# Two operand distances and one step of the FFN's order in a float32 decoder block

## The chip, the cores and the metric

The kernel runs on one core of a Trainium2 chip. The metric is the device time of one execution in microseconds; before the change the median of three runs is 378.98 us. The matrix engine is called PE or TensorE here, its weight loads PEld, the vector engine VectorE or DVE, the scalar engine ScalarE or ACT.

## What is computed

One decoder layer over 256 tokens of width 1024, in float32, cut to what matters:

```python
h = rms_norm(x, attn_norm_g)
proj = h @ w_in                      # qa ka va qb kb vb (512 columns each), 8 forget logits, 2048 gate logits
o_a = moba_attention(rope(norm(qa)), rope(norm(ka)), va)     # 8 heads of 64; one block of 256 keys: causal attention
o_b = forgetting_attention(norm(qb), norm(kb), vb, log_f)    # 8 heads, with a cumulative decay in the scores
gates = sigmoid(g_logit + b_gate)
x = x + (gates[0] * (o_a @ w_branch_moba) + gates[1] * (o_b @ w_branch_fox)) @ w_out
u, g = split(rms_norm(x, ffn_norm_g) @ w_ffn_up)             # 2 x 2816 columns
g = causal_depthwise_conv(g, ffn_conv_w) + ffn_conv_b        # width 3
x = x + (silu(g) * u) @ w_ffn_down
```

## The kernel before

**Products in three matmuls.** Every operand of a large product is split into two float32r tiles, a high part and a rest; a product is high × high, rest × high and high × rest. The splitting of weights is `load`: it fetches a chunk of 1 MB into `raw` (a ring of RB = 3 buffers), then for each half of the chunk ScalarE copies the high part to `whi` (L124) and VectorE subtracts for `wlo` (L125); both have rings of HB = 6 slots of 4096 bytes a partition. `use(c, h)` asks for a half, and lets `load` run AHEAD = 5 halves in front. Chunks are fetched in the order of the list `chunks`; all weights' fetches are issued on one queue (SP).

**Which operand is stationary.** A matmul holds one tile of 128 columns in the array (loaded by PEld) and streams the other past it.
- `project_lead` (L225) and `project` (L235), which make q, k, v: x (`xh`, `xl`) is stationary, 512 columns of `whi` or `wlo` are streamed.
- `twin` (L445 to L447), for the gates and for `up` of the FFN; the branch projections (L541 to L543); the output projection (L568 to L570); `down` (L637 to L639): the weights are stationary, 256 columns of activations are streamed. These stand in `xh`, `xl`, `oh`, `ol` and, for `down`, in `qA`, `qB`, `kA`, which belong to the attention before.
- the norm of the FFN (L596): `onesr` stationary, `sqr` streamed.

**Addresses.** Tiles lie in SBUF one behind the other as they are first named. `gap0` of GAPS[0] bytes, the twelve slots of `whi` and `wlo`, and `onesr` come first, then `gap1` of GAPS[1] bytes, then x's tiles, `oh`, `ol`, `qA`, `qB`, `kA` and `sqr`, all of sizes that are multiples of 1024 bytes. The slots start at 4384 (32 modulo 256) and `xh` at 54240 (224 modulo 256). All slices taken for a matmul start at multiples of 512 bytes from there, so streamed minus stationary is 192 modulo 256 wherever weights are stationary, 64 where x is, and 0 in the scores of the attention (`qA` or `qB` against `kA`, L385, L386).

**Order.** PE runs in the order in which the program names its matmuls; the other engines follow their data. The attention's small steps (transposes L280 and L408, scores L385 and L386, values L419) are put between the projections and the gates by hand. In the FFN, `up(f)` makes 128 columns of u and of g in 48 matmuls, `activate(f)` brings them from PSUM (L606) through the convolution and silu to the tiles that `down` streams (L618, L619), and `down(p)` takes two such f in 48 matmuls. `norm2` runs inside `up(1)`, so that `activate(0)` and `activate(1)` come after it. The order of the steps is u0 u1 u2 u3 d0 u4 u5 d1 u6 u7 d2 and so on. `down` holds five of the eight PSUM banks, which leaves three for `up`.

Of the kernel before, what the change touches and what calls it, by code (L numbers as in the profile page):

```python
# [9 lines left out]
F32R = mybir.dt.float32r  # L10
# [7 lines left out]
P = 128  # L18
S = 256
NT = 2  # L20
D = 1024
KT = D // P
HD = 64
NH = 8
W4 = 512
DFF = 2816
NF = DFF // P
# [2 lines left out]
HALF = 8  # L30
RB, HB, AHEAD = 3, 6, 5
NWARM = 9
GAPS = (160, 192)
LW = S + 2 * W4


C_G2, C_BG, C_CW, C_CB, C_QG, C_BF, C_GR = 0, 8, 24, 90, 112, 116, 124
C_END = 156


@with_exitstack
def decoder_block(ctx, tc, a, out):
# [7 lines left out]
    def T(shape, tag, bufs=1, dt=F32):  # L50
        return sb.tile(shape, dt, tag=tag, bufs=bufs, name=tag)

    def bank():
        return ps.tile([P, 512], F32, tag="bank", bufs=8, name="bank")


    def gap(tag, n):
        nc.gpsimd.memset(T([P, n // 4], tag), 0.0)

    gap("gap0", GAPS[0])  # L60
    for tag in ("whi", "wlo"):
        T([P, 1024], tag, HB, F32R)
    T([P, P], "onesr", 1, F32R)
    gap("gap1", GAPS[1])
    for tag in ("xh", "xl", "oh", "ol"):
        T([P, KT, S], tag, 1, F32R)
# [8 lines left out]
    chunks = [("lead", j) for j in range(2)] + [("qkv", 0, 1), ("qkv", 1, 1)]  # L75
# [1 line left out]
    chunks += [("wg", c) for c in range(KT)]  # L77
    chunks += [("wb", c) for c in range(4)]
    chunks += [("wo", c) for c in range(4)]
    for j in range(NF // 2):  # L80
        chunks += [("wu", 2 * j), ("wu", 2 * j + 1)]
        if j > 0:
            chunks.append(("wd", j - 1))
    chunks.append(("wd", NF // 2 - 1))
    pos = {c: i for i, c in enumerate(chunks)}
    split = {}
    state = {"next": 0, "raw": None}

    def load(upto):
        while state["next"] <= min(upto, 2 * len(chunks) - 1):  # L90
            i, h = divmod(state["next"], 2)
            c = chunks[i]
            if h == 0:
                raw = state["raw"] = T([P, 2 * LW], "raw", RB)
                if c[0] == "lead":
                    cuts = (0, S + W4, LW, LW + S + W4, 2 * LW) if i == 0 else (0, LW, 2 * LW)
                else:
                    cuts = (0, 1024, 2048) if i < 4 else (0, 2048)
                src = a[c[0]]
                for j in c[1:]:  # L100
                    src = src[j]
                if i == 2:
                    nc.sync.dma_start(xT[:, 4:8], a["xT"][:, 4:8])
                for u, v in zip(cuts, cuts[1:]):
                    nc.sync.dma_start(raw[:, u:v], src[:, u:v])
            hi = T([P, 1024], "whi", HB, F32R)
            lo = T([P, 1024], "wlo", HB, F32R)
            if c[0] == "lead":
                k = 2 * i + h
                piece = state["raw"][:, h * LW:(h + 1) * LW]  # L110
                xk, raw = piece[:, 0:S], piece[:, S:]
                split_x(k, xk)
                nc.scalar.activation(xsq[0][:, k], xk, AF.Square)
                n = 2
            else:
                raw = state["raw"][:, h * 1024:(h + 1) * 1024]
                n = 1
                if i == 2:
                    for k in (4 + 2 * h, 5 + 2 * h):
                        split_x(k, xT[:, k])  # L120
            w = 1024 // n
            for j in range(n):
                s = slice(j * w, (j + 1) * w)
                nc.scalar.activation(hi[:, s], raw[:, s], AF.Copy)  # L124
                nc.vector.tensor_tensor(lo[:, s], raw[:, s], hi[:, s].bitcast(F32), op=ALU.subtract)  # L125
            split[c, h] = (hi, lo)
            state["next"] += 1

    def use(c, h):
        load(2 * pos[c] + h + AHEAD)  # L130
        if c == ("wb", 0) and h == 0:
            nc.sync.dma_start(xT[:, 0:4], a["xT"][:, 0:4])
        return split.pop((c, h))


    sm = T([P, C_END], "sm")
    g1 = T([P, KT], "g1")
    nc.scalar.dma_start(g1, a["g1"])

    def col(c, n=1):  # L140
        return sm[:, c:c + n]
# [7 lines left out]
    def split_x(k, x):  # L149
        g = g1[:, k:k + 1]  # L150
        if k == 0:
            nc.vector.tensor_scalar_mul(xh[:, k], x, g)
        else:
            nc.scalar.activation(xh[:, k], x, AF.Copy, scale=g)
        nc.vector.scalar_tensor_tensor(xl[:, k], x, g, xh[:, k].bitcast(F32), op0=ALU.mult, op1=ALU.subtract)
# [11 lines left out]
    load(5)  # L167
    nc.sync.dma_start(sm, a["smalls"])
    nc.scalar.activation(xsq[1], xT[:, 4:8], AF.Square)
    xss = T([P, 3, 512], "bias")  # L170
    nc.gpsimd.tensor_tensor(xss[:, 0], xsq[0][:, 0:2].rearrange("p k t -> p (k t)"), xsq[0][:, 2:4].rearrange("p k t -> p (k t)"), op=ALU.add)
    nc.gpsimd.tensor_tensor(xss[:, 1], xsq[1][:, 0:2].rearrange("p k t -> p (k t)"), xsq[1][:, 2:4].rearrange("p k t -> p (k t)"), op=ALU.add)
    nc.gpsimd.tensor_tensor(xss[:, 2], xss[:, 0], xss[:, 1], op=ALU.add)
# [6 lines left out]
    ones = cst[:, 256:384]  # L180
    mask3 = cst[:, 384:768]
    cos2 = cst[:, 768:832].rearrange("p (t c) -> p t c", t=NT)
    onesr = T([P, P], "onesr", 1, F32R)
    nc.scalar.activation(onesr, ones, AF.Copy)
    wfr = T([P, KT, NH], "wfr")
    nc.sync.dma_start(wfr, a["wf"])
# [30 lines left out]
    V = T([P, NT, 2 * W4], "V")  # L217
# [77 lines left out]
    bias = T([P, NH, 384], "bias")  # L295
# [129 lines left out]
    gates = T([P, KT, 2, S], "gates")  # L425
# [107 lines left out]
    for c in range(4):  # L533
        bp = banks()
        for br in range(2):
            wh, wl = use(("wb", c), br)
            for j in range(2):
                o = bp[j][:, br * S:(br + 1) * S]
# [5 lines left out]
        for j in range(2):  # L544
            b = 2 * c + j
# [12 lines left out]
    for c in range(4):  # L558
        for h in range(2):
            wh, wl = use(("wo", c), h)  # L560
            j = 2 * (c % 2) + h
            for i in range(2):
                b = 2 * j + i
                o = acc[b]
                for k4 in range(4):
                    k = 4 * (c // 2) + k4
# [32 lines left out]
    def up(f):  # L599
        up_ = bank()  # L600
        twin("wu", f, up_, hh, hl, f == 0, norm2 if f == 1 else None)
        return up_

    def activate(f, up_):
        ev = T([P, 2, S], "sq", 2)
        nc.vector.tensor_tensor(ev, up_.rearrange("p (b t) -> p b t", b=2), rs2[:, None, :].to_broadcast([P, 2, S]), op=ALU.mult)  # L606
        u, g = ev[:, 0], ev[:, 1]
        w = T([P, 3, S], "s", 3)
        cv, sl, av = w[:, 0], w[:, 1], w[:, 2]
        nc.scalar.activation(cv, g, AF.Identity, scale=col(C_CW + 2 * NF + f), bias=col(C_CB + f))  # L610
        nc.vector.scalar_tensor_tensor(cv[:, 1:], g[:, 0:S - 1], col(C_CW + NF + f), cv[:, 1:], op0=ALU.mult, op1=ALU.add)
        nc.vector.scalar_tensor_tensor(cv[:, 2:], g[:, 0:S - 2], col(C_CW + f), cv[:, 2:], op0=ALU.mult, op1=ALU.add)
        nc.scalar.activation(sl, cv, AF.Silu)
        nc.vector.tensor_tensor(av, u, sl, op=ALU.mult)
        if f % 2 == 0:
            acts[f // 2] = T([P, 4, S], ("qA", "qB", "kA")[f // 2 % 3], 1, F32R)
        ah, al = acts[f // 2][:, f % 2], acts[f // 2][:, 2 + f % 2]
        nc.scalar.activation(ah, av, AF.Copy)  # L618
        nc.vector.tensor_tensor(al, av, ah.bitcast(F32), op=ALU.subtract)  # L619
# [4 lines left out]
    def down(p):  # L624
        ac = acts.pop(p)
        last = p == NF // 2 - 1
        w2 = [use(("wd", p), h) for h in range(2)]
        order = [(h, d) for d in ((0, 1), (2, 3), (4, 5), (6,), (7,)) for h in range(2)] if last else [(h, (d,)) for h in range(2) for d in range(KT)]
        for h, ds in order:
            wh, wl = w2[h]  # L630
            ah, al = ac[:, h], ac[:, 2 + h]
            for d in ds:
                b = 4 if d == 7 else d // 2
                c = d % 2 if d < 6 else 0
                o = acc[b][:, c * S:(c + 1) * S]
                w = slice(d * P, (d + 1) * P)
                nc.tensor.matmul(o, wh[:, w], ah, start=(p == 0 and h == 0 and c == 0), stop=False)  # L637
                nc.tensor.matmul(o, wh[:, w], al, start=False, stop=False)  # L638
                nc.tensor.matmul(o, wl[:, w], ah, start=False, stop=(last and h == 1 and d == ds[-1]))  # L639
            if last and h == 1:  # L640
                n = len(ds)
                y = yy[:, ds[0]:ds[0] + n]
                nc.vector.tensor_tensor(y, acc[b][:, 0:n * S].rearrange("p (b t) -> p b t", b=n), x1[:, ds[0]:ds[0] + n], op=ALU.add)
                nc.sync.dma_start(out[:, ds[0]:ds[0] + n], y)

    for j in range(NF // 2):
        pair = []
        for f in (2 * j, 2 * j + 1):
            pair.append(up(f))
            if j > 0:  # L650
                activate(f, pair.pop())
        if j == 0:
            for f in range(2):
                activate(f, pair[f])
        if j > 0:
            down(j - 1)
    down(NF // 2 - 1)


def _layout(i):  # L660
# [19 lines left out]
    a["wd"] = c(i["w_ffn_down"][0].reshape(NF // 2, 2, P, D).transpose(0, 2, 1, 3).reshape(NF // 2, P, 2048))  # L680
    sm = np.empty((P, C_END), f)
    a["g1"] = c(i["attn_norm_g"][0].reshape(KT, P).T)
# [42 lines left out]
```

## Time and profile before

| | us |
|---|---|
| runs | 378.75, 378.98, 379.49 |
| the profiled execution | 379.49 |
| its span, first to last instruction | 377.7 |
| PE busy in it | 370.6 |
| DVE busy | 288.8 |
| ACT busy | 228.9 |
| mean granted TensorE clock | 1.000 |

The profile is of one execution, and its span leaves out what lies around the first and the last instruction. A matmul's own duration in it is partly modelled and spans more than two of its neighbours' starts; the pace is read from start to start, in the timeline, or from the count of matmuls in a stretch of the windows view. In views that name what waited, `L638 <- DVE qA L619` means that the matmul of line 638 began when the vector engine's instruction of line 619 had written `qA`.

### The profile page before, as it was taken

The page shows a single profiled execution, that of the slowest core. Times are in us where ns is not written, and L with a number is a line of the kernel's source. Part 1 is how long each engine was busy: PE and PEld are TensorE (multiplying, and loading weights), DVE is VectorE, ACT ScalarE, POOL GpSimd, SP SyncE. Part 2 cuts the span into 40 slices and gives each one's busy share as a digit, 9 for nine tenths or more (in the row PEclk, how much of TensorE's full clock was granted, in tenths as well). Part 3 has the DMA queues.
Part 4 walks back from the last instruction along what each step waited for, and adds up shares of the span by engine and source line. Part 5 has one row for each costly group of instructions (what it writes and reads, how often), then busy time and mean ns, then how long its engine had stood idle before and what let it go on. Part 6 is the DMA issues. An engine that isn't in the chain of part 4 may idle for free.

```text
span 377.7 us, 7097 instructions
## 1 busy us (share of the span) xinstructions
PE 370.6 (98%) x2893; PEld 349.4 (93%) x2893; DVE 288.8 (76%) x509; ACT 228.9 (61%) x387; POOL 15.4 (4%) x19
## 2 busy tenths in 40 slices
PE   8999999999899999999999999999999999999996
PEld 4787888889799989999999899999999999999996
DVE  4989989898997663886795978686766867677653
ACT  5947696759957794445577755555454646455430
POOL 2430000000000000000050000000000000000000
PEclk9999999999999999999999999999999999999999
DMA  8976622655156334454544545555564565546002
GB/s 268 411 268 252 252 111 95 241 193 209 52 217 211 125 113 150 186 183 159 217 162 174 219 147 194 222 180 172 208 222 164 180 215 210 175 179 220 0 2 111
DMA packets 11424, 68.63 MB, mean 182 GB/s; under 512 B 1528, under 2 KB 1920, under 8 KB 3968
## 3 DMA queue, kind: packets, MB, share of 16 engines
q1 hardware_dynamic: 11088, 67.13, 49.5%
q10 hardware_dynamic: 304, 1.06, 0.7%
q8 instruction: 22, 0.36, 0.4%
q14 instruction: 10, 0.08, 0.1%
HBM read 67.13 MB, written 1.06 MB: 181 GB/s over the span
## 4 chain that ended last, share of the span: by engine, by line
PE 73%; DVE 10%; ACT 9%; issue 3%; DMA 3%; SPq 0%; ACTq 0%; DVEq 0%
PE bank L445 13%; PE bank L447 12%; PE bank L446 12%; PE bank L638 5%; PE bank L639 5%; DVE wlo L125 5%; PE bank L637 5%; PE bank L235 4%; ACT whi L124 3%; PE bank L541 2%; PE bank L542 2%; PE bank L569 2%; PE bank L568 2%; PE bank L570 2%; PE bank L543 2%
## 5 line engine op out<-in xcount | busy, mean ns | idle before, releaser
L125 DVE TENSOR_TENSOR wlo<-raw,whi 128x1024 fp32r<-128x1024 f32 (+1 forms) x126 | 153.3, 1221 | 49.4 <-ACT whi L124 48.9
L124 ACT ACTIVATE whi<-raw 128x1024 fp32r<-128x1024 f32 (+1 forms) x126 | 128.7, 1029 | 82.3 <-PE bank L446 47.5
L445 PE MATMUL bank<-oh,whi 128*128 128x256 f32 x352 | 97.5, 277 | 0.0
L446 PE MATMUL bank<-ol,whi 128*128 128x256 f32 x352 | 97.5, 277 | 0.0
L447 PE MATMUL bank<-oh,wlo 128*128 128x256 f32 x352 | 97.5, 277 | 0.0
L446 PEld LDWEIGHTS bank<-ol,whi 128*128 128x128 f32 x352 | 66.2, 188 | 0.0
L445 PEld LDWEIGHTS bank<-oh,whi 128*128 128x128 f32 x352 | 66.2, 188 | 0.0
L447 PEld LDWEIGHTS bank<-oh,wlo 128*128 128x128 f32 x352 | 66.1, 188 | 0.0
L445 PE MATMUL bank<-xh,whi 128*128 128x256 f32 x128 | 36.3, 284 | 0.4 <-DVE qB L292 0.4
L447 PE MATMUL bank<-xh,wlo 128*128 128x256 f32 x128 | 35.7, 279 | 0.0
L446 PE MATMUL bank<-xl,whi 128*128 128x256 f32 x128 | 35.7, 279 | 0.0
L445 PEld LDWEIGHTS bank<-xh,whi 128*128 128x128 f32 x128 | 24.1, 189 | 1.5 <-issue 0.7
L235 PE MATMUL bank<-whi,xh 128*128 128x512 f32 x80 | 25.4, 399 | 0.0
L235 PE MATMUL bank<-wlo,xh 128*128 128x512 f32 x80 | 25.0, 394 | 0.2 <-DVE wlo L125 0.2
L235 PE MATMUL bank<-whi,xl 128*128 128x512 f32 x80 | 24.9, 392 | 0.0
L446 PEld LDWEIGHTS bank<-xl,whi 128*128 128x128 f32 x128 | 24.1, 188 | 0.0
L447 PEld LDWEIGHTS bank<-xh,wlo 128*128 128x128 f32 x128 | 24.1, 188 | 0.0
L606 DVE TENSOR_TENSOR sq<-bank,rs 128x512 f32<-128x512 f32 x22 | 15.1, 690 | 6.5 <-PE bank L447 6.5
L638 PE MATMUL bank<-qA,whi 128*128 128x256 f32 x64 | 17.8, 278 | 0.9 <-DVE qA L619 0.9
L235 PEld LDWEIGHTS bank<-wlo,xh 128*128 128x128 f32 x80 | 15.0, 188 | 3.9 <-DVE wlo L125 0.6
L394 ACT ACTIVATE s<-s,nm 128x128 f32<-128x128 f32 (+1 forms) x32 | 14.2, 448 | 6.6 <-DVE nm L391 6.6
L235 PEld LDWEIGHTS bank<-whi,xl 128*128 128x128 f32 x80 | 15.0, 188 | 3.4
(183 smaller groups left out, 781.7 us busy)
## 6 DMA issues: line engine op xcount, KB each, us to landing
raw<-in_wu SPq DMA_DIRECT2D x22, 1024.0 KB, 4.8
raw<-in_wd SPq DMA_DIRECT2D x11, 1024.0 KB, 4.8
raw<-in_qkv SPq DMA_DIRECT2D x8, 1024.0 KB, 4.9
raw<-in_wg SPq DMA_DIRECT2D x8, 1024.0 KB, 4.8
raw<-in_wb SPq DMA_DIRECT2D x4, 1024.0 KB, 4.8
raw<-in_wo SPq DMA_DIRECT2D x4, 1024.0 KB, 4.9
raw<-in_qkv SPq DMA_DIRECT2D x4, 512.0 KB, 8.0
raw<-in_lead SPq DMA_DIRECT2D x2, 640.0 KB, 7.2
```

Source lines behind the costliest of these rows:

```text
L124: nc.scalar.activation(hi[:, s], raw[:, s], AF.Copy)
L125: nc.vector.tensor_tensor(lo[:, s], raw[:, s], hi[:, s].bitcast(F32), op=ALU.subtract)
L235: nc.tensor.matmul(pt[t], lhs[:, k, t * P:(t + 1) * P], rhs, start=(k == 0 and i == 0), stop=(k == KT - 1 and i == 2))
L394: last_exp[:] = [nc.scalar.activation(s[:, j, c], s[:, j, c], AF.Exp, scale=-1.0, bias=nm[:, j, i:i + 1], accum_out=l[:, j, i:i + 1])]
L445: nc.tensor.matmul(o, wh[:, w], mh[:, k], start=(k == 0 and i == 0), stop=False)
L446: nc.tensor.matmul(o, wh[:, w], ml[:, k], start=False, stop=False)
L447: nc.tensor.matmul(o, wl[:, w], mh[:, k], start=False, stop=(k == KT - 1 and i == 1))
L541: nc.tensor.matmul(o, wh[:, w], oh[:, 4 * br + k], start=(k == 0), stop=False)
L606: nc.vector.tensor_tensor(ev, up_.rearrange("p (b t) -> p b t", b=2), rs2[:, None, :].to_broadcast([P, 2, S]), op=ALU.mult)
L637: nc.tensor.matmul(o, wh[:, w], ah, start=(p == 0 and h == 0 and c == 0), stop=False)
L638: nc.tensor.matmul(o, wh[:, w], al, start=False, stop=False)
L639: nc.tensor.matmul(o, wl[:, w], ah, start=False, stop=(last and h == 1 and d == ds[-1]))
```

## The change

The slots of `whi` and `wlo` grow to 4352 bytes (17 × 256), so that a half's 4096 bytes can start at one of two places in its slot: 16 bytes in where weights are stationary, 128 bytes in for the chunks `lead` and `qkv`, which are streamed; `onesr` starts 16 bytes in as well. With GAPS[1] = 128 the slots still start at 32 modulo 256, and `xh` and the tiles behind it at 160. Stationary weights are then at 48, and streamed tiles 112 bytes behind them; the streamed weights of q, k, v are at 160, x's own place, a distance of 0. The scores keep a distance of 0.

To make room, the ring `raw` has buffers of 8192 instead of 10240 bytes. The two leading chunks, which hold x beside weights and don't fit, go to the tiles of `gates` and of `bias`, which are not in use by then, and the sums of squares, which stood in `bias`, to the tile of `V`.

In the FFN the order becomes u0 u1 u2 u3 u4 d0 u5 d1 u6 u7 d2 and so on: `down(0)` comes after `up(4)` and `activate(4)`. The fetches follow the same list.

```diff
-GAPS = (160, 192)
+GAPS = (160, 128)
+W_STAY, W_STREAM = 4, 32
+WT = 1024 + 64
...
+def ffn_order():
+    steps = [(("wu", f), f) for f in range(5)] + [(("wd", 0), 0), (("wu", 5), 5), (("wd", 1), 1)]
+    for j in range(3, NF // 2):
+        steps += [(("wu", 2 * j), 2 * j), (("wu", 2 * j + 1), 2 * j + 1), (("wd", j - 1), j - 1)]
+    return steps + [(("wd", NF // 2 - 1), NF // 2 - 1)]
...
     for tag in ("whi", "wlo"):
-        T([P, 1024], tag, HB, F32R)
-    T([P, P], "onesr", 1, F32R)
+        T([P, WT], tag, HB, F32R)
+    T([P, WT - 1024 + P], "onesr", 1, F32R)
...
-    for j in range(NF // 2):
-        chunks += [("wu", 2 * j), ("wu", 2 * j + 1)]
-        if j > 0:
-            chunks.append(("wd", j - 1))
-    chunks.append(("wd", NF // 2 - 1))
+    chunks += [c for c, _ in ffn_order()]
...
-                raw = state["raw"] = T([P, 2 * LW], "raw", RB)
                 if c[0] == "lead":
+                    raw = T([P, KT, 2, S], "gates").rearrange("p k b t -> p (k b t)") if i == 0 else T([P, NH, 384], "bias").rearrange("p h t -> p (h t)")
...
                 else:
+                    raw = T([P, 2048], "raw", RB)
...
-            hi = T([P, 1024], "whi", HB, F32R)
-            lo = T([P, 1024], "wlo", HB, F32R)
+            o = W_STREAM if c[0] in ("lead", "qkv") else W_STAY
+            hi, lo = (T([P, WT], tag, HB, F32R)[:, o:o + 1024] for tag in ("whi", "wlo"))
...
-    xss = T([P, 3, 512], "bias")
+    xss = T([P, NT, 2 * W4], "V").rearrange("p t (j c) -> p (t j) c", j=2)
...
-    onesr = T([P, P], "onesr", 1, F32R)
+    onesr = T([P, WT - 1024 + P], "onesr", 1, F32R)[:, W_STAY:W_STAY + P]
...
-    for j in range(NF // 2):
-        pair = []
-        for f in (2 * j, 2 * j + 1):
-            pair.append(up(f))
-            if j > 0:
-                activate(f, pair.pop())
-        if j == 0:
-            for f in range(2):
-                activate(f, pair[f])
-        if j > 0:
-            down(j - 1)
-    down(NF // 2 - 1)
+    early = []
+    for (kind, _), n in ffn_order():
+        if kind == "wd":
+            down(n)
+            continue
+        early.append((n, up(n)))
+        if n > 0:
+            for e in early:
+                activate(*e)
+            early = []
```

More of the change, by code (lines that the diff above doesn't have):

```diff
@@ L93, in load @@
             if h == 0:
-                raw = state["raw"] = T([P, 2 * LW], "raw", RB)
                 if c[0] == "lead":
+                    raw = T([P, KT, 2, S], "gates").rearrange("p k b t -> p (k b t)") if i == 0 else T([P, NH, 384], "bias").rearrange("p h t -> p (h t)")
                     cuts = (0, S + W4, LW, LW + S + W4, 2 * LW) if i == 0 else (0, LW, 2 * LW)
                 else:
+                    raw = T([P, 2048], "raw", RB)
                     cuts = (0, 1024, 2048) if i < 4 else (0, 2048)
+                state["raw"] = raw
                 src = a[c[0]]
```

## The prediction

> **What bounds the kernel now.** I read the page first, then stretches of the windows view, then the timeline of the matrix engine, because the first two leave only the pace of single matmuls in question.
>
> ```profile
> span 377.7 us, 7097 instructions
> PE 370.6 (98%) x2893; PEld 349.4 (93%) x2893; DVE 288.8 (76%) x509; ACT 228.9 (61%) x387; POOL 15.4 (4%) x19
> PE 73%; DVE 10%; ACT 9%; issue 3%; DMA 3%; SPq 0%; ACTq 0%; DVEq 0%
> ```
>
> PE is busy for 98% of the span and carries 73% of the chain that ended last. So the time is the number of matmuls times the step from one start to the next, plus the few places where PE stops. The windows view, by stage (gates, branch and output projections, first four FFN chunks, the stop behind them, the rest of the FFN):
>
> ```profile
> core 0: us, PE busy (x) PEld busy (x) DVE busy (x) ACT busy (x) POOL busy (x), PEclk, DMA share, GB/s
> 87.00:147.00 60.00, 59.01 (x510) 55.80 (x506) 45.25 (x101) 46.38 (x101) 0.00 (x0) 1.00 0.45 159
> 147.00:192.40 45.40, 45.40 (x388) 45.30 (x385) 34.55 (x53) 24.20 (x36) 2.51 (x3) 1.00 0.49 176
> 192.40:215.30 22.90, 22.90 (x197) 22.90 (x195) 18.37 (x29) 16.98 (x24) 3.29 (x4) 1.00 0.48 172
> 215.30:217.00 1.70, 0.78 (x7) 0.58 (x6) 1.70 (x4) 1.62 (x3) 0.00 (x0) 1.00 0.93 390
> 217.00:374.50 157.50, 157.47 (x1390) 157.27 (x1388) 112.14 (x156) 77.53 (x111) 0.00 (x0) 1.00 0.47 165
> ```
>
> The clock is 1.00 in every stage, yet the pace is not one pace: a window also counts the two or three matmuls that began before it, so 45.40 us hold 386 (117.6 ns each) and 157.50 us hold 1388 (113.5 ns each), all of them 256 columns wide. The timeline gives the steps exactly. First and last of 191 steps in the branch projection:
>
> ```profile
> 147.33 0.28 PE L542 MATMUL bank<-ol,whi 128*128 128x256 f32 x1
> ...
> 169.82 0.28 PE L568 MATMUL bank<-xh,whi 128*128 128x256 f32 x1
> ```
>
> 22.49 us / 191 = 117.7 ns, which I call the slow step. First and last of 96 steps in the FFN:
>
> ```profile
> 221.99 0.28 PE L445 MATMUL bank<-oh,whi 128*128 128x256 f32 x1
> ...
> 232.87 0.28 PE L637 MATMUL bank<-qB,whi 128*128 128x256 f32 x1
> ```
>
> 10.88 us / 96 = 113.3 ns, the fast step. Both have the same distance of operands: streamed tiles start 192 bytes after the stationary weights modulo 256 (that is, 64 ahead of them). So the place alone does not pick the step. What switches it is a break; here is the one in the FFN, where `down(0)` waits for its activation:
>
> ```profile
> 215.17 0.28 PE L447 MATMUL bank<-oh,wlo 128*128 128x256 f32 x1
> 215.29 0.33 PE L637 MATMUL bank<-qA,whi 128*128 128x256 f32 x1
> 216.53 0.38 PE L638 MATMUL bank<-qA,whi 128*128 128x256 f32 x1 [0.92 <-DVE qA L619]
> 216.76 0.28 PE L639 MATMUL bank<-qA,wlo 128*128 128x256 f32 x1
> 216.87 0.29 PE L637 MATMUL bank<-qA,whi 128*128 128x256 f32 x1
> ```
>
> Before this break all four chunks of `up` ran at the slow step (22.90 us for about 194 matmuls, two of them the norm's: 118 ns); behind it everything to the end ran at the fast one. The eight gates show the same toss, one window inside each:
>
> ```profile
> 88.50:92.50 4.00, 4.00 (x37) 4.00 (x37) 3.62 (x9) 3.88 (x9) 0.00 (x0) 1.00 0.73 233
> 97.00:101.50 4.50, 4.50 (x41) 4.50 (x40) 4.30 (x7) 4.42 (x8) 0.00 (x0) 1.00 0.02 7
> 105.00:109.50 4.50, 4.50 (x42) 4.50 (x41) 4.46 (x17) 2.93 (x9) 0.00 (x0) 1.00 0.56 186
> 111.50:116.00 4.50, 4.50 (x41) 4.50 (x40) 3.43 (x15) 2.82 (x9) 0.00 (x0) 1.00 0.60 211
> 118.50:123.00 4.50, 4.50 (x41) 4.50 (x40) 3.43 (x15) 2.90 (x9) 0.00 (x0) 1.00 0.68 222
> 127.00:131.50 4.50, 4.50 (x40) 4.50 (x39) 1.97 (x9) 4.47 (x11) 0.00 (x0) 1.00 0.65 233
> 134.50:138.50 4.00, 4.00 (x38) 4.00 (x37) 1.60 (x3) 4.00 (x10) 0.00 (x0) 1.00 0.53 172
> 141.50:145.50 4.00, 4.00 (x38) 4.00 (x37) 1.16 (x2) 1.63 (x3) 0.00 (x0) 1.00 0.72 252
> ```
>
> With two or three taken off each count, the gates at 97, 111, 118 and 127 us are slow and the other four fast, whatever VectorE, ScalarE and the DMAs do meanwhile. The projections of q, k, v stream 512 columns and have two paces too:
>
> ```profile
> 24.42 0.63 PE L235 MATMUL bank<-whi,xh 128*128 128x512 f32 x2
> ...
> 28.16 0.62 PE L235 MATMUL bank<-whi,xl 128*128 128x512 f32 x2
> ...
> 44.43 0.62 PE L235 MATMUL bank<-whi,xl 128*128 128x512 f32 x2
> ...
> 48.55 0.62 PE L235 MATMUL bank<-whi,xl 128*128 128x512 f32 x2
> ```
>
> 3.74 us / 16 = 233.8 ns, and 4.12 us / 18 = 228.9 ns. Most are of the second kind; 230 is my mean.
>
> **The change, part by part.** *The places.* Every 256-column product against stored weights moves from 192 to 112 bytes. These are 384 matmuls of gates, 192 of branch, 192 of output, 1056 of `up`, 528 of `down`, together 2352; slow now are 4 × 48 in the gates, 192, 192 and 4 × 48 in `up`: 768. No row has 112 bytes, so I bound it. Upper end of the step: 117.7, the slow one. Lower end: the transposes, which load 128 columns of weights each and stream only 128:
>
> ```profile
> 132.16 0.66 PE bank L408 x6
> ```
>
> 0.66 / 6 = 110 ns; no matmul with a full load of weights follows another sustainedly in less. Between these ends, the rows nearest to other distances are those of the forget gate, whose stationary slice moves on by 64 bytes from one k to the next (first and last of 12 steps):
>
> ```profile
> 29.30 0.28 PE L306 MATMUL bank<-xh,wf 128*16 128x256 f32 x1
> ...
> 30.70 0.28 PE L306 MATMUL bank<-xh,wf 128*16 128x256 f32 x1
> ```
>
> 1.40 / 12 = 116.7 ns over four distances, though only 16 columns of weights are loaded. So no distance seen goes below the fast step, and I take 113.3 for all 2352: 768 × 4.4 ns = 3.4 us gained. The ends: 2352 at 110 gain 768 × 7.7 + 1584 × 3.3 = 11.1 us; all at 117.7 lose 1584 × 4.4 = 7.0 us.
>
> *q, k, v.* Weights and x get the same place, distance 0, where 64 was. The scores have distance 0 now and keep it (three steps of 256 columns):
>
> ```profile
> 64.16 0.28 PE L386 MATMUL bank<-kA,qB 128*128 128x256 f32 x1
> ...
> 64.51 0.63 PE L235 MATMUL bank<-whi,xh 128*128 128x512 f32 x2
> ```
>
> 0.35 / 3 = 117 ns, twice that 234 for 512 columns: by this row 288 × 4 = 1.2 us are lost; at twice the 110 of the transposes 288 × 10 = 2.9 us are won. I take 0, as today's mixture lies between.
>
> *The FFN's order.* `down(0)` moves behind `up(4)`, and `activate(4)` with its loads ahead of it; `down(1)` stays behind `up(5)`. The stop costs 216.53 − 215.29 − 0.12 = 1.12 us, and the next step 0.11 more than usual: 1.23 us. It ended when VectorE wrote the second activation:
>
> ```profile
> 207.95 1.28 DVE L606 TENSOR_TENSOR sq<-bank,rs 128x512 f32<-128x512 f32 x2
> 216.06 0.75 DVE L619 TENSOR_TENSOR qA<-s,qA 128x256 fp32r<-128x256 f32 x2
> ```
>
> `up(4)` puts 48 matmuls, 5.4 to 5.7 us, between; its bank is the one that the second L606 frees at 209.2 us, six microseconds early, and the activation is done at 216.8, four ahead of `down(0)`'s new start at some 220.7. Nothing else is late next: VectorE is busy 112 of 157 us behind that. The weights' chunks are reordered with the steps, so no queue waits on a step that comes later: 1.23 us gained, 0 if another wait takes its place.
>
> *Buffers.* The two leading chunks leave the ring of three, so the second chunk of q, k, v needn't wait for the first to be split:
>
> ```profile
> 4.11 0.96 SPq L105 DMA_DIRECT2D raw<-in_qkv  x2
> 9.11 0.80 SPq L105 DMA_DIRECT2D raw<-in_qkv  x2
> ```
>
> It can then be issued some microseconds before 9.11. PE is idle for 7.1 us of the whole span (377.7 − 370.6) and in the lead for next to nothing, so I cost this at nothing; if the earlier transfer slowed the leading ones, it would cost some tenths of a microsecond. The sums of squares move into V's tile, which ScalarE first writes much later:
>
> ```profile
> 42.60 1.27 ACT V L239 x2
> ```
>
> The norm that reads them runs before the first projection of V begins; also nothing.
>
> Sum: −3.4 − 1.2 = −4.6 us on the profiled execution, which took 379.49 us (span 377.7 and 1.8 around it). That execution is the slowest of three; the median is 378.98, so 374.4 us.
>
> **The rivals.** *The stretch goes altogether.* 113.3 may be a fast step with some collision left. The change's distance is the first that is not a multiple of 32 bytes, and all rows above are such multiples: that speaks for it; against it, that sixteen columns of weights stretch the step as much as 128 do. At 110 and 220 ns it gives 11.1 + 2.9 + 1.2 = 15.2 us: 363.8. The Trainium skill's page "TensorE: Matmul & The Clock Gate", section "Back-to-back issue gap", gives columns / 2.4 + 2.5 ns for a warm matmul, 109.2 and 215.8 here; by it the sum would be 360.5. The trace does not agree for today's places (113.3 at best).
>
> *The slow step for good.* The break that the new order removes is the one behind which the pace became fast. If the pace is drawn at a break and then kept, all of `up` and `down` inherit what the gates and projections ran at. For it: slow from 147 to 215 us without a change, across four stages. Price: 864 + 528 = 1392 matmuls × 4.4 = 6.1 us, less 1.2: 383.9. It decides from about 280 such matmuls on. Against it: at 112 bytes there may be one step only.
>
> *The places do nothing.* The same page, in "What happens when you issue a matmul", says that loading the next weights takes no read bandwidth from the running matmul, through a second port. By such a mechanism the distance can't matter, and only the stop goes, with the paces as they are drawn today: 377.7. The two steps at one distance speak neither way.
>
> **How the numbers follow.** A measurement of this kernel tells about 0.2% (0.8 us) from no change. Chances: forecast, 371 to 376.5, 0.36; no stretch or half of it, 360 to 371, 0.23; only the stop, 377.7 (0.34% faster), 0.09; slow step in most of the FFN, 380 to 385, 0.26; gains and losses that cancel, within 0.2%, 0.06. So faster 0.67, same 0.06, slower 0.27. The range 362 to 384 leaves out about 0.05 below and 0.09 above; the forecast's own is 371 to 376.5.
>
> **What would show it.** The stop at 215 us is gone, and `L638 <- DVE qA L619` with it. 150 us of the FFN hold some 1324 matmuls: more than 1335 would be the first rival, under 1285 the second. Windows in the gates and from 147 to 192 us show 117.7 replaced by 113.3; if they still toss between both, the place is not the cause. For q, k, v, 18 matmuls in 4.1 us mean no change. Wrong throughout would be a PE that now waits on `wlo` in 20 to 90 us, where VectorE has little slack.

## The result, and the profile after

| | us, median | ratio to before, 95% interval |
|---|---|---|
| before | 379.24 | |
| after | 382.69 | 1.0093 [1.0073, 1.0113] |

The change makes the kernel 3.4 us slower; I had forecast 4.6 us faster. Five of 42 executions of the kernel before took 384.9 to 385.5 us, three of ten of `e5_old192` (below) 385.0 to 385.5, and one of four of `e4_180` 618.36 at a granted clock of 0.56; they are left out of the ratios and have no profile, but 6 us is also what the slow step costs in the FFN. The profiled execution of the changed kernel (`after` from here on) took 382.66 us, and its page says that PE is still everything:

```profile
span 380.9 us, 7095 instructions
PE 375.1 (98%) x2893; PEld 355.1 (93%) x2893; DVE 288.5 (76%) x509; ACT 229.4 (60%) x387; POOL 15.3 (4%) x19
PE 86%; ACT 7%; DVE 4%; DMA 1%; issue 1%; ACTq 0%
```

The same 2893 matmuls, and 4.5 us more of busy PE. The stop in the FFN is gone; here is the edge from `up(4)` to `down(0)` in the timeline (line numbers are 11 higher than before):

```profile
220.56 0.28 PE L458 MATMUL bank<-oh,wlo 128*128 128x256 f32 x1
220.68 0.28 PE L648 MATMUL bank<-qA,whi 128*128 128x256 f32 x1
220.80 0.28 PE L649 MATMUL bank<-qA,whi 128*128 128x256 f32 x1
```

But the pace behind it is not the old one. In the windows view (projections, the first four `up`, where the stop was, the rest):

```profile
147.50:192.00 44.50, 44.50 (x384) 44.46 (x382) 33.94 (x52) 23.63 (x36) 2.52 (x3) 1.00 0.51 175
192.50:215.00 22.50, 22.50 (x195) 22.50 (x195) 18.45 (x29) 17.02 (x24) 3.30 (x4) 1.00 0.49 170
215.00:217.00 2.00, 2.00 (x20) 2.00 (x19) 2.00 (x5) 1.58 (x3) 0.00 (x0) 1.00 1.02 430
217.00:374.00 157.00, 157.00 (x1348) 157.00 (x1348) 109.62 (x152) 77.82 (x111) 0.00 (x0) 1.00 0.46 162
```

With two or three off each count, 44.50 / 382 and 157.00 / 1346 are 116.5 and 116.6 ns: from 147 us to the end there is one pace, 116.6 to 116.7 from start to start, and it is neither the fast step of before (113.3) nor its slow one (117.8). The gates are worse, one window inside each of the first four:

```profile
88.00:92.00 4.00, 4.00 (x36) 4.00 (x35) 3.54 (x9) 3.87 (x8) 0.00 (x0) 1.00 0.70 242
97.00:101.00 4.00, 4.00 (x35) 4.00 (x35) 3.80 (x7) 3.92 (x7) 0.00 (x0) 1.00 0.00 0
105.00:109.00 4.00, 4.00 (x36) 4.00 (x34) 3.96 (x14) 2.72 (x9) 0.00 (x0) 1.00 0.39 129
111.50:115.50 4.00, 4.00 (x37) 4.00 (x36) 2.93 (x15) 2.81 (x9) 0.00 (x0) 1.00 0.52 172
```

33 or 34 steps in 4 us; from start to start in the timeline they are 119.9, 119.9, 119.9 and 118.4 ns, and over all eight gates the mean rises from 115.7 to 119.3. Only q, k, v gain (12 steps in the timeline):

```profile
12.37 0.62 PE L236 MATMUL bank<-whi,xl 128*128 128x512 f32 x2
...
15.09 0.62 PE L236 MATMUL bank<-whi,xl 128*128 128x512 f32 x2
```

2.72 us / 12 = 226.7 ns where the mean was 230; the first half chunk behind a stop takes up to 233, and the mean of all is 228.

The terms, from the paces of the two profiles: projections and the first four `up` 576 × (117.8 → 116.7) = −0.6; gates 384 × (115.7 → 119.3) = +1.4; rest of the FFN 1392 × (113.3 → 116.7) = +4.7; q, k, v 288 × (230 → 228) = −0.6; the stop −1.2. Together +3.7; the span grew by 3.2, the median by 3.45.

### The profile page after: what moved, and what is told of

It reads as the page before. It is cut to its first block, busy times and chain, and to the rows that moved or that the text cites. A ratio compares the mean times of both kernels' runs of the same rounds, so it can differ in the third digit from the quotient of the medians.

```text
span 380.9 us, 7095 instructions
## 1 busy us (share of the span) xinstructions
PE 375.1 (98%) x2893; PEld 355.1 (93%) x2893; DVE 288.5 (76%) x509; ACT 229.4 (60%) x387; POOL 15.3 (4%) x19
## 4 chain that ended last, share of the span: by engine, by line
PE 86%; ACT 7%; DVE 4%; DMA 1%; issue 1%; ACTq 0%
PE bank L456 14%; PE bank L457 14%; PE bank L458 14%; PE bank L246 9%; PE bank L649 5%; PE bank L650 5%; PE bank L648 5%; PE bank L236 3%; PE bank L552 2%; PE bank L580 2%; PE bank L579 2%; PE bank L553 2%; PE bank L581 2%; PE bank L554 2%; ACT whi L135 2%; DVE wlo L136 2%
## 5 line engine op out<-in xcount | busy, mean ns | idle before, releaser
L136 DVE TENSOR_TENSOR wlo<-raw,whi 128x1024 fp32r<-128x1024 f32 x118 | 146.9, 1248 | 49.4 <-ACT whi L135 48.0
L135 ACT ACTIVATE whi<-raw 128x1024 fp32r<-128x1024 f32 x118 | 124.2, 1056 | 84.0 <-PE bank L457 49.4
L456 PE MATMUL bank<-oh,whi 128*128 128x256 f32 x352 | 98.2, 279 | 0.0
L552 PE MATMUL bank<-oh,whi 128*128 128x256 f32 x64 | 18.0, 281 | 0.0
```

The lines of the kernel that those rows point to most:

```text
L456: nc.tensor.matmul(o, wh[:, w], mh[:, k], start=(k == 0 and i == 0), stop=False)
L552: nc.tensor.matmul(o, wh[:, w], oh[:, 4 * br + k], start=(k == 0), stop=False)
```

## The experiments

Two things could have done it. The distance theory: 112 bytes has a step of its own, some 116 to 120 ns. The break theory (my second rival): the order removed the break behind which the pace became fast, whatever the distance. I call it a draw when the pace behind a stop is one of several that the distance is seen to have, and nothing known beforehand says which. First each half of the change alone, and two sweeps over the distance. The paces below are start to start in the timeline; the windows shown give the same with two or three off each count.

**The order alone**

```diff
-    chunks += [("wu", 2 * j), ("wu", 2 * j + 1)] ...   # in before.py
+    chunks += [c for c, _ in ffn_order()]              # and the steps likewise; places stay as before
```

> The kernel before with the new FFN order alone; operand distances stay 192 (stationary weights) and 64 (q, k, v). Distance theory (the places made the change slower, and a pace once taken is kept until a break): no pace but 113.3 and 117.7 ns per 256-column matmul shows; the stop at 215 us is gone, so the FFN keeps the pace of the output projection: 383.9 us if that is 117.7, 377.7 if it is 113.3. Order theory (the order made the change slower, by whatever it does to PE): slower than before by 3 us or more, with a pace of 116.7 in the FFN.

Measured 384.25 us, 1.0132 [1.0115, 1.0149]. Windows in the branch projection and in the FFN, of this kernel:

```profile
150.00:168.00 18.00, 18.00 (x155) 18.00 (x154) 14.63 (x23) 8.67 (x12) 0.00 (x0) 1.00 0.50 176
220.00:370.00 150.00, 150.00 (x1276) 150.00 (x1275) 105.16 (x144) 75.07 (x106) 0.00 (x0) 1.00 0.48 169
```

and the FFN of `before`, in the same view:

```profile
220.00:370.00 150.00, 150.00 (x1326) 150.00 (x1325) 106.64 (x147) 75.97 (x109) 0.00 (x0) 1.00 0.48 169
```

50 matmuls fewer in 150 us. The stop is gone, and the slow step, 117.8 ns, goes on from 147 us to the end. This is my second rival to 0.4 us (383.9).

**The places alone**

```diff
-    chunks += [c for c, _ in ffn_order()]
+    for j in range(NF // 2): ...                       # the old list and the old loop of steps
```

> The changed kernel with the FFN's old order; distances 112 and 0. Distance theory: 116.7 ns from 147 us to the end as in the changed kernel, before and behind the stop, which comes back with its 1.2 us: 383.9 us. Order theory: the stop sets the FFN back to 113.3 ns, about 378 us or less.

Measured 388.51 us, 1.0234 [1.0207, 1.0261]. The stop is back in its timeline, and the windows before and behind it (205 and 220 us) differ:

```profile
215.46 0.28 PE L652 MATMUL bank<-qA,whi 128*128 128x256 f32 x1
216.56 0.39 PE L653 MATMUL bank<-qA,whi 128*128 128x256 f32 x1 [0.82 <-DVE qA L634]
```

```profile
205.00:213.00 8.00, 8.00 (x71) 8.00 (x70) 7.07 (x12) 6.05 (x8) 0.00 (x0) 1.00 0.36 132
220.00:370.00 150.00, 150.00 (x1270) 150.00 (x1269) 104.21 (x142) 74.50 (x106) 0.00 (x0) 1.00 0.48 169
```

116.7 ns ahead of the stop, 118.3 behind it. Neither expectation held: 383.9 and 1392 × 1.7 ns = 2.3 us more make 386.2, near the profiled execution. So a break redraws the pace at 112 too, but none of its draws, 116.7, 118.3 or (in the gates) 120.0, is 113.3. In the two profiles with 112 throughout none of 16 gates ran at 113.3; in six profiles with 192 (`before` and five of the runs in this section) 24 of 48 did. The profiled execution is the shortest of four (386.44); the other three took 2 us more and have no profile.

So both are true: the order leaves the FFN without a redraw, and 112 showed no fast step to draw. Either half alone makes the kernel slower. By medians the places are worth −1.6 us under the new order (384.25 to 382.69), and +9.3 under the old (+7.2 for the profiled execution).

**Which distances have a fast step?** Three kernels keep the order and the buffers of `after` and move the weights' place from chunk to chunk; the third also moves all tiles by 64 bytes.

```diff
-            o = W_STREAM if c[0] in ("lead", "qkv") else W_STAY
+            o = 4 * (i % 16) if i < 12 else 4 * ((i - 12) % 16) if i < 28 else 4 * ((i - 28) // 2 % 16)        # s1_up
+            o = 60 - 4 * (i % 16) if i < 12 else 60 - ... if i < 28 else 60 - 4 * ((i - 28) // 2 % 16)         # s2_down
+            o = 26 + i if i < 12 else 16 + i - 12 if i < 28 else 40 + (i - 28) // 2                            # s3_fine
-GAPS = (160, 128)
+GAPS = (224, 128)                                                                                          # s3_fine
```

> The changed kernel with another start of the weights in their slots for every chunk: in q, k, v a distance of 128, 144, 160 and so on by 16 bytes from chunk to chunk; in gates and projections 128, 112, 96 and so on down, one chunk each; in the FFN the same, two chunks each. Distance theory: the pace changes at the chunk's edge, without any break between chunks, with 116.7 at 112 and one of 113.3 and 117.7 at 192; some distances may be under 113. Carried-pace theory (a pace drawn at a break stays, whatever the distance): one pace from 147 us to the end.

> As the run with rising starts, with the starts falling from chunk to chunk, so that each distance is entered from its other neighbour. Distance theory: the same pace at the same distance as with rising starts, but for distances that have two paces. Carried-pace theory: one pace from 147 us to the end.

> The changed kernel with all tiles 64 bytes further on, and distances by 4 bytes: q, k, v from -24 to 20 around 0; gates and projections from 64 down to 4, one chunk each; FFN from 224 down to 160, two chunks each. Distance theory: 113.3 ns at 192 though stationary and streamed tiles lie elsewhere, 118.3 at 224, 116.7 around 32 to 48, and the finer steps show how wide the good places are. Absolute-place theory (the tiles' own addresses modulo 256 decide): 192 is nothing special now, and all paces of the earlier sweeps stand 64 bytes off.

One execution each: 386.68, 386.05 and 385.80 us. Windows of `s1_up` at distances 112, 48, 208, 192 and 176:

```profile
206.50:214.50 8.00, 8.00 (x70) 8.00 (x69) 7.26 (x12) 6.08 (x8) 0.00 (x0) 1.00 0.37 132
252.50:260.50 8.00, 8.00 (x70) 8.00 (x70) 5.32 (x7) 4.07 (x6) 0.00 (x0) 1.00 0.44 142
321.00:329.00 8.00, 8.00 (x71) 8.00 (x70) 4.99 (x8) 3.91 (x6) 0.00 (x0) 1.00 0.45 138
331.00:339.00 8.00, 8.00 (x73) 8.00 (x72) 6.68 (x10) 4.62 (x8) 0.00 (x0) 1.00 0.46 167
343.00:351.00 8.00, 8.00 (x69) 8.00 (x69) 5.21 (x6) 3.46 (x4) 0.00 (x0) 1.00 0.44 142
```

and of `s3_fine`, 7 us each, at 204, 192, 188, 184, 180, 176 and 168:

```profile
255.00:262.00 7.00, 7.00 (x64) 7.00 (x63) 4.33 (x6) 3.18 (x5) 0.00 (x0) 1.00 0.58 188
288.00:295.00 7.00, 7.00 (x64) 7.00 (x63) 4.26 (x7) 3.81 (x5) 0.00 (x0) 1.00 0.57 165
298.00:305.00 7.00, 7.00 (x61) 7.00 (x60) 5.81 (x10) 3.48 (x6) 0.00 (x0) 1.00 0.45 150
310.00:317.00 7.00, 7.00 (x62) 7.00 (x61) 4.08 (x6) 3.51 (x4) 0.00 (x0) 1.00 0.49 159
321.00:328.00 7.00, 7.00 (x64) 7.00 (x63) 4.51 (x7) 3.62 (x5) 0.00 (x0) 1.00 0.45 154
331.00:338.00 7.00, 7.00 (x61) 7.00 (x61) 5.84 (x9) 3.61 (x6) 0.00 (x0) 1.00 0.46 157
356.00:363.00 7.00, 7.00 (x64) 7.00 (x63) 4.29 (x6) 3.30 (x5) 0.00 (x0) 1.00 0.00 0
```

64 against 60 to 62 in 7 us: 113.3 ns at 168, 180, 192 and 204, twelve bytes apart, and 117.8 to 120.2 at all others between. All 40 distances seen in the runs of this document, by the mean over the second half of each chunk, halves with a wait left out (the distances lie 4 bytes apart from 4 to 64 and from 160 to 224, and 16 elsewhere):

| step, ns | distances, bytes |
|---|---|
| 113.3 | 168, 180, 192, 204 |
| 116.5 to 117.5 | 32, 44, 48; at times 16, 112, 160, 168 |
| 117.6 to 118.9 | 8, 24, 60, 64, 80, 128, 164, 184, 188, 200, 208, 212, 224, 240; at times 112, 160, 176, 192 |
| 119.3 to 120.5 | 0, 4, 12, 20, 28, 36, 40, 56, 96, 144, 172, 196, 216, 220; at times 16, 112, 128, 176 |
| 123.4 | 52 |

Some distances had two or three paces in different chunks; nothing went under 113.3. The twelve bytes do not go on at 216 (119.3); 156 was not tried. 192 was fast at two pairs of places modulo 256 (stationary 32 and streamed 224 in `before` and `s3_fine`, 224 and 160 in `s1_up` and `s2_down`), and at 48, 64, 176, 208 and 224 the steps of `s1_up` and of `s3_fine`, whose tiles lie 64 bytes further on, agree within 0.2 ns; so it is the distance that counts. The slots of the weights stand 17 × 256 bytes apart and share one step, so it counts modulo 256; not modulo 64 or 128, as 192 can be fast and 64 and 128 were not. The pace changed at the edge between two chunks, where PE does not stop, so a pace is not simply carried on. Two details of the expectations were wrong: 112 gave 118.4 to 120.0 here and not 116.7, and between 32 and 48 the step rises to 120.

**192 with the changed buffers, and edges.** If only the distance counts, the buffers and the order of `after` with 192 should behave as `e1_order`; and if an edge works as a break does, one half chunk at another distance would set the FFN to fast.

```diff
-W_STAY, W_STREAM = 4, 32
+W_STAY, W_STREAM = 48, 32                                       # e3_192
+            if (c, h) in ((("wb", 0), 0), (("wu", 2), 0)):
+                o = 52                                          # b1_edge: 176 for these two halves
```

> The changed kernel with W_STAY = 48: stationary weights at a distance of 192 again, q, k, v at 0, new FFN order. Distance theory: 113.3 or 117.7 from 147 us to the end by the draw at the last break, 374 or 383.5 us, nothing between; q, k, v 0.7 us shorter than before. Absolute-place or slot-size theory: another pace.

> As the run with W_STAY = 48, but the first half chunk of the branch projection and of the third FFN chunk stand at a distance of 176. In the sweeps the edge into 192 gave 113.3 each of the five times. If an edge sets the pace and the pace is then kept: 117.7 nowhere behind 150 us and 374 to 375 us, over 1% faster than before. If the edge only draws the pace: as without it, 374 or 383.5.

384.54 us, 1.0145 [1.0127, 1.0164], and 384.18, 1.0129 [1.0113, 1.0145]. The FFN of the two:

```profile
220.00:370.00 150.00, 150.00 (x1276) 150.00 (x1275) 104.92 (x144) 74.80 (x105) 0.00 (x0) 1.00 0.48 169
```

```profile
220.00:370.00 150.00, 150.00 (x1276) 150.00 (x1275) 104.88 (x144) 74.75 (x105) 0.00 (x0) 1.00 0.49 169
```

The first is `e1_order` again: q, k, v's place, the ring and the moved buffers make no measurable difference there. The second is a miss of mine: behind both edges the step was 117.8, although edges into 192 had led to 113.3 in the sweeps. An edge does not set the pace dependably.

**The old order with 192 and the changed buffers**

```diff
+W_STAY, W_STREAM = 48, 32                                       # and the old order, as in e2_places
```

> The changed kernel with W_STAY = 48 and the FFN's old order: distance 192 for stationary weights, 0 for q, k, v, and the stop at 215 us is there again. If the stop is what gave the kernel before its 113.3 ns in the FFN: 117.7 up to the stop, 113.3 behind it, and some 378.5 us, less than before by what q, k, v gain (0.7 us). If it only draws: 378.5 or 385.

379.25 us, 1.000 [0.9989, 1.0010]. Windows ahead of the stop and behind it:

```profile
194.00:214.00 20.00, 20.00 (x173) 20.00 (x172) 15.76 (x24) 14.92 (x20) 1.71 (x3) 1.00 0.45 161
220.00:370.00 150.00, 150.00 (x1326) 150.00 (x1325) 106.30 (x147) 75.49 (x108) 0.00 (x0) 1.00 0.47 169
```

The slow step, the stop, then the fast one, as before. Both times that the expectation gives for a stop that only draws were measured, 379 and 385 us; without a profile of the long ones, a slow draw at the stop is not shown. With the buffers and q, k, v's place of `after` the total is the same, so these parts are worth nothing that can be measured. Against `e3_192` the order alone costs 5.3 us at this distance.

**A distance that was only seen fast: 180**

```diff
+W_STAY, W_STREAM = 51, 32                                       # e4_180: new order; e6_old180: old order
```

> The changed kernel with W_STAY = 51: distance 180, which showed 113.3 ns in the fine sweep, new order. If 180 has the fast pace alone: 113.3 from 147 us to the end, 373.5 us. If it has two paces as 192 has: about 384.

> Distance 180 with the FFN's old order, so that the pace can't change with the order. If the order is worth the stop and nothing else: 113.3 ns before and behind the stop, and 1.2 us more than with the new order, 376.8 us. If the stop draws a pace at 180 too: some runs at 117.7 to 118.3 behind it, 383 us.

With the new order 375.56 us, 0.9897 [0.9874, 0.9920]; with the old 376.93, 0.9928 [0.9916, 0.9941]. New order: gates, branch projection, first `up`, FFN:

```profile
88.00:92.00 4.00, 4.00 (x37) 4.00 (x36) 4.00 (x9) 3.89 (x10) 0.00 (x0) 1.00 0.57 195
97.00:101.00 4.00, 4.00 (x38) 4.00 (x37) 3.83 (x6) 3.95 (x7) 0.00 (x0) 1.00 0.00 0
150.00:168.00 18.00, 18.00 (x161) 18.00 (x160) 15.66 (x24) 8.88 (x13) 0.00 (x0) 1.00 0.53 189
194.00:214.00 20.00, 19.85 (x175) 19.66 (x174) 16.08 (x25) 15.25 (x21) 1.44 (x2) 1.00 0.55 191
220.00:370.00 150.00, 150.00 (x1326) 150.00 (x1326) 106.34 (x146) 74.03 (x105) 0.00 (x0) 1.00 0.48 168
```

113.3 in every stage, once settled (the first half of a gate takes up to 115.0). The time is 2 us above the 373.5 expected; 0.4 us of it is a wait in `up(0)`, between the starts at 194.56 and 195.21 us, which kernels with a slower step there do not meet, and I have not traced the rest. Old order, timeline of the stop, and the FFN in the windows view:

```profile
212.94 0.38 PE L652 MATMUL bank<-qA,whi 128*128 128x256 f32 x1
214.24 0.39 PE L653 MATMUL bank<-qA,whi 128*128 128x256 f32 x1 [0.92 <-DVE qA L634]
```

```profile
220.00:370.00 150.00, 150.00 (x1326) 150.00 (x1326) 105.62 (x145) 74.68 (x106) 0.00 (x0) 1.00 0.48 166
```

At 180 the pace is the same on both sides of the stop, and what the order gains is the stop itself: 376.93 − 375.56 = 1.4 us (1.2 by the two ratios).

**Does an edge between two fast distances cost, or help?**

```diff
+W_STAY, W_STREAM = 48, 32                                       # both
+            o = ... else (45, 48, 51, 54)[i % 4]                # b2_cycle: 204, 192, 180, 168 in turn
+            if c in (("wb", 0), ("wo", 3), ("wu", 2)):          # b3_edge208: 192, these chunks at 208
+                o = 44
```

> The changed kernel with distances 204, 192, 180, 168 in turn, chunk by chunk, for all stationary weights; each showed 113.3 ns in the fine sweep when entered over an edge. If an edge sets the pace and these four are good places: 113.3 in nearly all chunks and 374 us. If an edge draws between the two: a mixture of 113.3 and 117.7 to 118.5, 378 to 381 us.

> Distance 192 with one whole chunk at 208 ahead of the branch projection, at the output projection's end and in the third FFN chunk. From 208 the edge into 192 gave 113.3 both times in the sweep (from 176 it failed in the run with half chunks). If the neighbour that is left decides: 113.3 behind each edge, 374 to 375 us. If it is a draw: 117.7 behind some, 376 to 384.

`b2_cycle` took 375.14 us, 0.9895 [0.9880, 0.9911], the lowest here, though not told apart from `e4_180`: every chunk at 113.3 once settled, also those at 192, except one gate at 168 with 116.7. `b3_edge208` came in two kinds, 376.5, 376.6 and 377.1 us, and 382.9, its profiled one (median 376.82, 0.9934 [0.9917, 0.9952]). Windows of that one, behind the first edge, behind a short wait in `up(0)`, and in the FFN behind the last edge:

```profile
154.00:162.00 8.00, 8.00 (x73) 8.00 (x72) 6.98 (x13) 4.31 (x7) 0.00 (x0) 1.00 0.36 131
197.00:206.00 9.00, 9.00 (x79) 9.00 (x78) 5.25 (x9) 6.75 (x8) 0.00 (x0) 1.00 0.47 173
220.00:370.00 150.00, 150.00 (x1276) 150.00 (x1275) 104.27 (x143) 74.28 (x106) 0.00 (x0) 1.00 0.47 166
```

113.3, then 117.8, and 117.8 to the end. Here is where the step changed, inside a chunk at 192:

```profile
195.26 0.28 PE L458 MATMUL bank<-oh,whi 128*128 128x256 f32 x1
195.47 0.39 PE L459 MATMUL bank<-ol,whi 128*128 128x256 f32 x1
195.70 0.28 PE L460 MATMUL bank<-oh,wlo 128*128 128x256 f32 x1
```

PE lost 0.2 us over these two steps; ahead of them the step is 113.3, behind them 117.7, and the norm's own two matmuls at 199.35 us change nothing. So the step changed at a wait far shorter than the stop of 1.1 us. Of the three edges from 208 into 192, two gave 113.3 and the last 117.8: an edge draws too. Between the two kinds lie 6 us, as many as 1392 matmuls × 4.4 ns = 6.2; the short ones have no profile, so that their FFN ran fast is inferred from this.

## Why the prediction was wrong

- *The places* is the step that failed: 113.3 ns for all 2352 matmuls, −3.4 us. I took a step measured at 192 for a distance of 112, and called the upper end 117.7. At 112 the runs show 116.7, 118.3 and 120.0. The rows to hand pointed that way: the forget gate's, 116.7 ns over four distances, and the scores', 117 at 0. I used the first only to say that nothing goes below the fast step. With 116.7 in the sum, 768 × 1.0 are gained and 1584 × 3.4 lost, +4.6; less the stop, +3.4 us: what was measured. That it came so close is partly chance, as the gates were worse and q, k, v better. The upper end was wrong too: 120.0, not 117.7.
- *The FFN's order* was right in mechanism and size: the stop went, `up(4)` covers it, nothing waits anew in `after`, and it is worth 1.2 to 1.4 us at 180 (1.23 forecast). But I put down the break's redraw as a rival and not as a term of the order: at the distance of `before` the order costs 5 us (`e1_order`, `e3_192`). This second omission alone would have turned the forecast's sign.
- *q, k, v* at 0: 2 ns a step shorter in the mean (229.8 to 227.8), 0.6 us in the profile, nothing measurable in `e5_old192`. At 64 the pace is drawn as well: `e1_order`, which keeps 64, has a mean of 231.6. *Buffers*: nothing, as forecast.
- *The slow step for good* is right for 192 (384.25 against 383.9), and in `after` only in direction: one pace is kept to the end, but it is 112's own. My sign of it, under 1285 matmuls in 150 us, is missed by the window of `after` by about one:

```profile
220.00:370.00 150.00, 150.00 (x1288) 150.00 (x1287) 105.71 (x145) 75.33 (x107) 0.00 (x0) 1.00 0.49 169
```

- *The stretch goes altogether* found no support: at 40 distances no step was under 113.3. The 109.2 ns that I took from the Trainium skill's page "TensorE: Matmul & The Clock Gate", section "Back-to-back issue gap", which gives it for an isolated matmul, was not reached.
- *The places do nothing* is refuted: moving only the stationary weights took the step from 113.3 ns (at 192) to 123.4 (at 52). The section "What happens when you issue a matmul" of the same page of the Trainium skill says that a weight load takes no read bandwidth from the running matmul; here the measurement decides, and the step does depend on where the two operands stand to each other.
- *Slips without weight*: the transposes' row is a piece of the chain of work; from start to start they follow at 108.6 ns, not 110. And the sum with 109.2 and 215.8 ns is 360.6, not 360.5.
- The forecast's time was about right for a kernel with the fast step throughout: 374.4 against 375.6 (180) and 375.1 (the cycle).

**Open.** Why the fast places lie 12 bytes apart and what picks the pace at a break are not settled. That 180 has only the fast step rests on nine executions in two orders, of which two have a profile, and on its chunks in `s3_fine` and `b2_cycle`; the one gate at 168 that ran at 116.7 shows that a fast place can draw another pace.

## What to carry to other kernels

Where PE is busy for 98% and the clock is full, read the step from start to start in every stage: a pace that differs between stages with the same instructions is a term of its own, and it can be carried on until PE stops or the distance changes. Before taking a stop out, look whether the pace changes behind it; before taking a distance, measure its step, and do not lend it one from another distance. A sweep of one offset from chunk to chunk measures a dozen distances in one run.

## What the hardware showed that I had not expected

- The step of a 128 × 128 × 256 float32r matmul depends on where the streamed tile starts relative to the weights, modulo 256: 113.3 to 123.4 ns over 40 distances at a granted clock of 1.00.
- At the same distance the pace can be one of two (113.3 or 117.8 at 192) and stays for hundreds of matmuls; a stop redraws it (once the step changed where PE lost 0.2 us, in `b3_edge208`), an edge between distances sometimes. With 512 columns the steps were 226.7 ns at distance 0 once settled and up to 239 elsewhere (244, in `s3_fine`).
